# Seven products on six k-tiles instead of four, in a hybrid decoder step on one core

## The chip, the core and the metric

The kernel runs on one core of a Trainium2 chip. What is compared is the device time of one launch in microseconds (us). Of the kernel before there are three timed runs, with a median of 3048.79 us (3048.49 to 3049.93), and one profiled execution of 3050.04 us, whose span from the first to the last instruction is 3048.2 us. Its rows stand below. PE is the matrix engine, PEld its weight loads, DVE the vector engine, ACT the scalar engine, SP the engine that issues the DMAs.

## What is computed

One decoder layer on a prompt of 2048 tokens and on 8 sampled tokens, all in fp32:

```python
xn = rms_norm(x, g_pre)                       # (tokens, 1024)
proj = einsum('bld,de->ble', xn, w_in)        # 1024 -> 11280 columns: the largest product
# columns: q, k, v of 8 delta-rule heads | z_a | a, b | q, k, v of 3 groups x 4 heads | z_b | gates
p_a = gated_delta_rule(silu(conv4(q, k, v)), g, beta) ...  @ w_proj_a
p_b = dilated_window_attention(3 groups)           ...  @ w_proj_b
h   = sigmoid(gate_a) * p_a + sigmoid(gate_b) * p_b
y   = x + rms_norm(h @ w_out, g_post)
```

The outputs are y of both token sets, the final delta-rule states, the last rows before the convolution, and keys and values.

## The kernel before

**Split operands.** Each fp32 operand of a large product is held as two fp32r parts, hi (a cast) and lo (the rest), and a product of a k-tile is three matmuls: hi x hi, hi x lo, lo x hi. In the code this is `three` in `step` (L991).

**The projection.** It is done in two halves of 1024 tokens. The weight columns are cut into 88 tiles of 128, which are worked on in pairs (44 pairs a half; the first pair of half 0 is done plainly in `opening`, with the a/b columns). For a pair the output is a 2 x 2 block: two column tiles by two token groups of 512 (in half 0 each group is done in pieces of 256 and 260 columns, the 4 more being sampled tokens; in half 1 in one piece of 512). The contraction has eight k-tiles of 128. On `KS` = 4 of them the block product is taken with Winograd's seven products of sums instead of eight products, each over `KH = KS // 2` = 2 k-tiles; on the other four (the "rest") it is taken plainly, two column tiles by two token groups. So a pair issues, for each piece, 7 x 2 x 3 = 42 matmuls of the seven products and 4 x 4 x 3 = 48 of the rest. `step` (L983) writes out their order: product 1, the rest that the pair before left over, products 7, 6, 2, rest, 5, 4, rest, 3, rest. In rows `xs1` to `xs7` are the sums of x that the products read, `xp4` to `xp7` the k-tiles of the rest, and `wh`/`wl` the hi and lo parts of the weights.

**What the products need.** On the x side `prep` loads and scales the tokens, `transposed1` and `sums` form the sums of x on DVE, `transpose` turns them on PE, and `xevac` splits them from PSUM (a cast on ACT or DVE, a subtraction on DVE). That is done once a half. On the weight side `wsplit` forms, for each pair, the sums of the weight blocks and splits them (`wput`: a cast on ACT or DVE, a subtraction on DVE) into one of six slots of 512 columns; a slot is freed when its last product is issued (`done` in `step`).

**What sets the order.** The order is settled at build time by a list scheduler (`Scheduler`), which runs generators as tasks with priorities. The projection is the task of lowest priority, and the work on finished tiles (delta rule, attention, gates, sampled tokens) is laid between its matmuls. Tiles are kept in 17 pages of SBUF; claims of pages (`claim`, `admitter`) are granted strictly in the order that the string `ORDER` gives, in which each letter is a delta-rule head, an attention head, a gate tile, and so on. Each engine then executes its own list in that fixed order. After the projection the output products (`final`) run in four token groups.

Of the kernel before, what the change touches and what calls it, by code (L numbers as in the profile page):

```python
# [17 lines left out]
T = 2048  # L18
# [8 lines left out]
KS = 4  # L27
# [426 lines left out]
def build(nc, tc, ctx, I, O):  # L454
# [18 lines left out]
    NPAGE = 17  # L473
# [3 lines left out]
    wslots = Pool([(tl(f"wh{i}", [128, 512], F32R), tl(f"wl{i}", [128, 512], F32R)) for i in range(6)])  # L477
    tbuf = tl("wt", [128, 2 * KH, 128])
# [8 lines left out]
    szg = tl("szg", [128, 12, NB])  # L487
# [79 lines left out]
    def xsamples(pg):  # L567

        page = yield Acquire(pages, 1)
        fxs = page[:, :96].rearrange("p (k t c) -> p k t c", t=2, c=4)  # L570
# [27 lines left out]
    def prep(hf, b, admit):  # L598
# [11 lines left out]
        def scales():  # L610
            st["s2"] = yield Acquire(pages, 1)
            g = I["g_pre"]
            yield K.load(st["s2"][:, :w], bass.AP(tensor=g.tensor, offset=g.offset, ap=[[0, 128], [1, w]]))
# [14 lines left out]
        def scale(i, r):  # L628
            yield K.stt(pg[i][:, :w], pg[i][:, :w], r, st["s2"][:, :w], OP.mult, OP.mult)
            yield K.scaled(pg[i][:, w:D], pg[i][:, w:D], r, ("act",))  # L630
# [57 lines left out]
    def transpose(hf, st, keys, summed=None):  # L688
        pg, m = st["pg"], 128 * KH
        for key in keys:  # L690
            if key[0] in (7, 6, 3):
                yield Wait(summed)
            if hf == 1:
                yield Wait(xfree[key])
            bank = yield Acquire(side, 1)
            if key[0] == "p":
                src = [pg[4 * key[2] + i][:, 128 * key[1]:128 * key[1] + 128] for i in range(4)]
            else:
                n, k = key
                o = 128 * k + m * (n in (2, 3, 4))  # L700
                if n == 6:
                    src = [st["s2"][:, m * i + o:m * i + o + 128] for i in range(4)]
# [30 lines left out]
    def sums(st, ev):  # L733
        m = 128 * KH
        for i in range(4):
            p, q, s2 = st["pg"][i], st["pg"][4 + i], st["s2"][:, m * i:m * i + m]
            a11, a12, s1, a22 = p[:, :m], p[:, m:2 * m], q[:, :m], q[:, m:2 * m]
            yield K.tt(s2, s1, a11, OP.subtract)
            yield K.tt(a11, a22, s2, OP.subtract)
            yield K.tt(a12, a12, s2, OP.subtract)  # L740
        ev.set()

    def transposed1(hf, st, toks):
# [5 lines left out]
        S.spawn(sums(st, ev := Event()), 5, f"sums{hf}")  # L749
# [4 lines left out]
        pages.release(*(pg[i] for i in range(4, 8)), st["s2"])  # L754
        tok.release(*toks, st["toks"][4])
# [3 lines left out]
        if hf == 0:  # L759
            yield Wait(xs_ev[1])  # L760
            pages.release(pg[8])
            tok.release(*st["toks"][5:])
# [25 lines left out]
    def wput(src, ev):  # L788

        hi, lo = slot = yield Acquire(wslots, 1)  # L790
        n = src.shape[1]
        yield K.copy(hi[:, :n], src)
        yield K.tt(lo[:, :n], src, hi[:, :n].bitcast(F32), OP.subtract)
        ev.set(slot)

    def wsplit():
        for at, (kind, us, evs) in enumerate(jobs):
# [4 lines left out]
            if kind == "ab":  # L802
# [3 lines left out]
                slot = yield Acquire(wslots, 1)  # L806
# [5 lines left out]
            elif kind == "plain":  # L812
                m = 128 * KH
                for j in range(2):
                    yield from wput(f[j][:, :2 * m], evs[j])
                    yield from wput(f[j][:, 2 * m:], evs[2 + j])
                T = tbuf.rearrange("p a b -> p (a b)")
                for j in range(2):
                    yield K.tt(T[:, m * j:m * j + m], f[j][:, m:2 * m], f[j][:, :m], OP.subtract)
                yield from wput(T[:, :2 * m], evs[4])  # L820
            elif kind == "pair":
# [3 lines left out]
                T = tbuf.rearrange("p a b -> p (a b)")  # L825
                t1, t2 = (T[:, m * j:m * j + m] for j in range(2))
                yield from wput(f[0][:, :2 * m], evs[0])
                yield K.tt(t1, b12, b11, OP.subtract)
                yield K.tt(b12, b22, b12, OP.subtract)
                yield from wput(f[1][:, :2 * m], evs[1])  # L830
                yield K.tt(t2, b22, t1, OP.subtract)
                yield from wput(T[:, :2 * m], evs[2])
                yield from wput(r1, evs[3])
                yield K.tt(b21, b21, t2, OP.subtract)
                yield from wput(b21, evs[4])
                yield from wput(r2, evs[5])
            else:
                if at < len(jobs) - 2:
                    for j in range(2):
                        yield from wput(f[0][:, 512 * j:512 * j + 512], evs[1 + j])  # L840
# [14 lines left out]
    def sink(t, th, gi, c0, n, bank, pool):  # L855
# [43 lines left out]
        if t.left == 0:  # L899
# [4 lines left out]
            elif k == "z" and t.half == 0:  # L904
                yield K.pcopy(szg[:, t.idx, :], pg[:, HT:HT + NB])
# [21 lines left out]
    def opening(work):  # L927
# [3 lines left out]
        for th in range(2):  # L931
# [36 lines left out]
    def inproj(hf, work):  # L968
# [14 lines left out]
    def step(hf, tiles, evs, slots, gi, c0, w, end, last):  # L983
# [7 lines left out]
        def three(acc, key, hl, off, first, final):  # L991
            hi, lo = (x[:, off:off + 128] for x in hl)
# [5 lines left out]
        def product(acc, n, slot, off, first=False):  # L998
            hl = yield from wk(slot)
            for k in range(KH):  # L1000
                yield from three(acc, (n, k), hl, off + 128 * k, first and k == 0, k == KH - 1)
                if last:
                    if hf == 0:
                        xfree[n, k].set()
                    else:
# [12 lines left out]
        def done(*ns):  # L1018
            if end:
                wslots.release(*(slots[n] for n in ns))  # L1020
# [66 lines left out]
    seb = tl("seb", [128, 2, GH, NB])  # L1087

    def ab_tables(hf, t, work):
# [62 lines left out]
        if hf == 0:  # L1152
# [9 lines left out]
            yield K.copy(seb.rearrange("p a h b -> p (a h b)"), bank[:, :128])  # L1162
            side.release(bank)
        pages.release(ab, pg, tmp, cmat)
# [9 lines left out]
    def conv(t):  # L1174
        pg = yield Wait(t.done)
        cp = yield Acquire(pages, 1)
# [4 lines left out]
        yield K.act(pg[:, :HT], c, AF.Tanh, scale=0.5)  # L1181
        yield K.stt(c, pg[:, :HT], 1.0, c, OP.add, OP.mult)
        pages.release(pg)
        return cp
# [27 lines left out]
    def gdn(hf, h, tk, tq, tv, tz, work, done):  # L1212
# [57 lines left out]
        tok.release(toks.pop())  # L1270
# [3 lines left out]
        tok.release(toks.pop())  # L1274
# [41 lines left out]
    def gdn_q(tq, kT, e, row, sm, tb, h, ev):  # L1316
        qT = yield from conv(tq)
        gp = yield Acquire(pages, 1)
        yield K.load(gp[:, :HT], bass.AP(tensor=row.tensor, offset=row.offset, ap=[[0, 128], [1, HT]]))
# [24 lines left out]
        pages.release(gp)  # L1344
# [385 lines left out]
    def wcols(slot, off, n):  # L1730

        o = off % 512
        return [x[:, o:o + n] for x in slot[off // 512]]
# [182 lines left out]
    def sample_gdn(tiles, abdone):  # L1916
# [25 lines left out]
        pg = yield Acquire(pages, 1)  # L1942
        for i in range(2):
# [42 lines left out]
        for h in range(GH):  # L1986
            S.spawn(sample_head(h, vn, sg_t, pg, kq, qk_b, os_, left, all_done), 15, f"sample{h}")
# [13 lines left out]
        yield K.tt(os_, os_, szg[:, 0:8], OP.mult)  # L2001
# [5 lines left out]
    def sample_head(h, vn, sg_t, pg, kq, qk_b, os_, left, all_done):  # L2007
# [47 lines left out]
    def sample_attn(tiles):  # L2055
# [10 lines left out]
        for h in range(4):  # L2066
            row = brow_d[h, BT:]
            yield K.load(nbs[8 * h:8 * h + 8], bass.AP(
                tensor=row.tensor, offset=row.offset, ap=[[0, NB], [4 * (BT + BS), 3], [1, BS]]))
        slog = pg[:, 908:1004].rearrange("p (g h b) -> p g h b", g=3, h=4)  # L2070
# [79 lines left out]
        yield K.stt(w[0], w[0], 0.5, szg[:, 8:12].rearrange("p h b -> p (h b)"), OP.mult, OP.mult)  # L2150
# [6 lines left out]
    def conv_state():  # L2157
# [13 lines left out]
    ORDER = ("GZaaGaZaGaagZGgaZagGZaagGagagZGagaZGaZagggggggxgyg",  # L2171
             "gGgZggaagGaZSagGaZaGaZgaggGaagTZGaZaCggGaaZgGZaggag")
    for hf in range(2):
# [12 lines left out]
        if hf == 0:  # L2186
            preps = [[claim(7), claim(4)], None]
# [5 lines left out]
        def add_gdn():  # L2193
# [6 lines left out]
            work = claim(4)  # L2200
# [21 lines left out]
        for what in ORDER[hf]:  # L2222
            if what in "GZag":
                {"G": add_gdn, "Z": add_gdn_gate, "a": add_attn, "g": add_gate}[what]()
            elif what == "x":
                preps[1] = [claim(5)]
# [126 lines left out]
```

## Time and profile before

| what | value |
|---|---|
| median of 3 runs | 3048.79 us |
| profiled execution | 3050.04 us |
| its span | 3048.2 us |
| PE busy | 3010.0 us (99%) |
| PEld busy | 2692.0 us (88%) |
| DVE busy | 2199.2 us (72%) |
| ACT busy | 1212.9 us (40%) |

PE is busy nearly all the time in every stage. Busy time of an engine is the union of its instructions' intervals; consecutive matmuls overlap in the records, so the cost of one more matmul is read from the distance of their starts and not from their duration. The projection of half 0 ends at about 1289 us and that of half 1 at about 2560 us; the output products follow.

### The profile page before, as it was taken

Reading aid. Unit: us, or ns where it says so; the run is one execution under the profiler, and the core shown is the slowest. Engines: PE = TensorE matmul, PEld = TensorE weight load, DVE = VectorE, ACT = ScalarE, POOL = GpSimd, SP = SyncE. Lnnn points to the kernel's source line nnn. Section 1 sums busy time; section 2 is a strip of 40 time slices with the busy share of each in tenths; the row PEclk is TensorE's granted clock in tenths of the full one; section 3 lists DMA queues with packets and bytes.
Section 4 is the critical chain, followed back from the end, with each engine's and each line's share of the span. In section 5 each row is a group of like instructions: output and inputs, shape, how many; then the busy total and the mean of one; then the engine's idle time right before and its main releaser. Section 6 shows DMA issues by size and latency. Waiting matters only on the chain.

```text
span 3048.2 us, 55885 instructions
## 1 busy us (share of the span) xinstructions
PE 3010.0 (99%) x20879; PEld 2692.0 (88%) x20879; DVE 2199.2 (72%) x5978; ACT 1212.9 (40%) x3444; POOL 141.1 (5%) x239
## 2 busy tenths in 40 slices
PE   7999999999999999999999999999999999999999
PEld 7999999999999999978887888888888888897887
DVE  6777767786778686767586868597988486666765
ACT  5545444344435443433442534343434343313121
POOL 1000000000000000000000000000000000000000
PEclk9999999999999999999999999999999999999999
DMA  4323242332233325332244332336452236565463
GB/s 125 94 73 89 58 112 71 99 85 83 70 98 89 89 79 147 110 85 81 73 121 124 88 88 80 105 96 186 137 158 86 76 100 180 176 204 197 149 226 117
DMA packets 468760, 343.46 MB, mean 113 GB/s; under 512 B 88745, under 2 KB 411825, under 8 KB 468480
## 3 DMA queue, kind: packets, MB, share of 16 engines
q1 hardware_dynamic: 468488, 339.89, 38.1%
q8 instruction: 164, 2.69, 0.4%
q14 instruction: 108, 0.88, 0.1%
HBM read 261.40 MB, written 80.97 MB: 112 GB/s over the span
## 4 chain that ended last, share of the span: by engine, by line
PE 94%; DVE 3%; DMA 2%; ACT 1%; issue 0%; SPq 0%; POOL 0%; DVEq 0%; POOLq 0%; ACTq 0%
PE bank L251 89%; PE bank L267 5%; DVE pg L311 1%; DMA wr<-in_w_in 0%; DVE wl L316 0%; DVE pg L316 0%; SPq L400 0%; DMA pg<-in_cache_v_w 0%; DMA pg<-in_x_prompt 0%; DMA pg<-in_state_gdn 0%; DMA pg<-gate 0%; ACT L280 0%; DMA ghh<-in_g_head_norm 0%; DVE wh L355 0%; DVE junk L311 0%
## 5 line engine op out<-in xcount | busy, mean ns | idle before, releaser
L280 ACT ACTIVATE pg<-bank 128x256 f32<-128x256 f32 (+7 forms) x741 | 331.8, 460 | 759.4 <-PE bank L251 690.0
L316 DVE TENSOR_TENSOR wl<-wr,wh 128x512 fp32r<-128x512 f32 x595 | 383.5, 647 | 21.3 <-ACT wh L280 3.3
L355 DVE CAST wh<-wr 128x512 fp32r<-128x512 f32 (+1 forms) x384 | 153.0, 399 | 206.9 <-PE bank L251 184.0
L251 PE MATMUL bank<-xp7s,wh 128*128 128x512 f32 (+3 forms) x1196 | 302.1, 328 | 0.0
L251 PE MATMUL bank<-xp6s,wh 128*128 128x512 f32 (+3 forms) x1132 | 290.1, 330 | 0.0
L251 PE MATMUL bank<-xp5s,wh 128*128 128x256 f32 (+3 forms) x1100 | 276.3, 327 | 0.0
L280 ACT ACTIVATE wh<-wr 128x512 fp32r<-128x512 f32 (+1 forms) x213 | 129.8, 611 | 351.9 <-PE bank L251 292.1
L251 PE MATMUL bank<-xp4s,wh 128*128 128x260 f32 (+2 forms) x1068 | 267.5, 326 | 1.6 <-DVE xp4s L311 1.6
L316 DVE TENSOR_TENSOR bank<-bank,etmp 128x256 f32<-128x256 f32 (+2 forms) x260 | 134.9, 519 | 129.4 <-PE bank L251 126.3
L251 PEld LDWEIGHTS bank<-xp7s,wh 128*128 128x128 f32 x1196 | 198.4, 188 | 17.5 <-issue 1.7
L251 PEld LDWEIGHTS bank<-xp6s,wh 128*128 128x128 f32 (+1 forms) x1132 | 189.2, 188 | 17.2 <-issue 0.8
L251 PEld LDWEIGHTS bank<-xp5s,wh 128*128 128x128 f32 (+1 forms) x1100 | 183.0, 188 | 14.7 <-issue 0.2
L251 PE MATMUL bank<-xp7s,wl 128*128 128x512 f32 (+3 forms) x592 | 195.0, 329 | 0.0
L251 PEld LDWEIGHTS bank<-xp4s,wh 128*128 128x128 f32 x1068 | 176.1, 188 | 14.9 <-DVE xp4s L311 1.8
L280 ACT ACTIVATE prob<-bank 128x512 f32<-128x512 f32 (+4 forms) x224 | 105.2, 482 | 208.7 <-PE bank L251 120.8
L311 DVE SCALAR_TENSOR_TENSOR pg<-pg,convw,pg 128x1024 f32<-128x1024 f32 x144 | 183.9, 1277 | 2.8 <-ACT pg L280 1.3
L251 PE MATMUL bank<-xp6s,wl 128*128 128x512 f32 (+2 forms) x560 | 184.9, 330 | 0.0
L251 PE MATMUL bank<-xp5s,wl 128*128 128x512 f32 (+2 forms) x544 | 178.5, 328 | 0.0
L251 PE MATMUL bank<-xs1k,wh 128*128 128x512 f32 (+4 forms) x708 | 177.8, 334 | 0.0
L251 PE MATMUL bank<-xp4s,wl 128*128 128x256 f32 (+2 forms) x528 | 172.5, 327 | 0.0
L251 PE MATMUL bank<-xs6k,wh 128*128 128x512 f32 (+3 forms) x680 | 171.3, 334 | 0.0
L251 PE MATMUL bank<-xs7k,wh 128*128 128x512 f32 (+3 forms) x680 | 169.9, 333 | 0.0
(302 smaller groups left out, 7474.8 us busy)
## 6 DMA issues: line engine op xcount, KB each, us to landing
wr<-in_w_in SPq DMA_DIRECT2D x176, 512.0 KB
pg<-in_x_prompt SPq DMA_DIRECT2D x32, 512.0 KB
pg<-grow SPq DMA_DIRECT2D x32, 512.0 KB
wr<-in_w_proj_a SPq DMA_DIRECT2D x32, 512.0 KB
wr<-in_w_out SPq DMA_DIRECT2D x32, 512.0 KB
pg<-og SPq DMA_DIRECT2D x24, 520.0 KB
pg<-gate SPq DMA_DIRECT2D x24, 512.0 KB
out<-pg SPq DMA_DIRECT2D x20, 512.0 KB
```

The costliest lines, as they stand in the source:

```text
L251: nc.tensor.matmul(out, lhsT, rhs, start=start, stop=stop, skip_group_check=shared)
L267: nc.tensor.transpose(out, in_, ident[:k, :k])
L280: return ("act", c, lambda: nc.scalar.activation(out, in_, func, **kw))
L311: lambda: nc.vector.scalar_tensor_tensor(out, in0, scalar, in1, op0=op0, op1=op1, **kw))],
L316: return ("dve", self._vcost(out, in0, in1), lambda: nc.vector.tensor_tensor(out, in0, in1, op=op))
L355: alts.append(("dve", self._vcost(out, in_, fast=True), lambda: nc.vector.tensor_copy(out, in_)))
```

## The change

`KS` goes from 4 to 6, so each of the seven products runs over three k-tiles and the rest has two. The x sums become 21 rows and the rest 4 (before 14 and 8). The six equal weight slots of 512 columns become three of 768 columns, one of 384 and two of 256, each kind with its own pool, and the scratch `tbuf` is gone: the sums of weights are formed in place in the loaded block. To make room the pages go from 17 to 15, two small tables (`szg`, `seb`) move to DRAM and are loaded where they are used, the convolution works in place over halves of 512 columns with a small buffer instead of a second page, `gdn_q` takes its row from the buffer of the inverse (`lanes`) instead of a page, and a delta-rule head claims 3 pages of work instead of 4, keeping the pages of its q and v. In `sums` the eight subtractions that products 7 and 6 need come first and have an event of their own; the four for product 3 follow. `ORDER` is a new string.

```diff
-KS = 4
+KS = 6
-    NPAGE = 17
+    NPAGE = 15
...
-    wslots = Pool([(tl(f"wh{i}", [128, 512], F32R), tl(f"wl{i}", [128, 512], F32R)) for i in range(6)])
-    tbuf = tl("wt", [128, 2 * KH, 128])
+    wslots, wthird, wrest = Pool([]), Pool([]), Pool([])
+    for i, (pool, w) in enumerate([(wslots, 256 * KH)] * 3 + [(wthird, 128 * KH)] + [(wrest, 128 * (8 - KS))] * 2):
+        pool.free.append((tl(f"wh{i}", [128, w], F32R), tl(f"wl{i}", [128, w], F32R), pool))
...
-    def sums(st, ev):
+    def sums(st, evs):
...
-            yield K.tt(s2, s1, a11, OP.subtract)
-            yield K.tt(a11, a22, s2, OP.subtract)
-            yield K.tt(a12, a12, s2, OP.subtract)
-        ev.set()
+            yield K.tt(s2, q[:, :m], p[:, :m], OP.subtract)
+            yield K.tt(p[:, :m], q[:, m:2 * m], s2, OP.subtract)
+        evs[0].set()
+        for p, q, s2 in tt:
+            yield K.tt(p[:, m:2 * m], p[:, m:2 * m], s2, OP.subtract)
+        evs[1].set()
...
             elif kind == "pair":
...
-                yield K.tt(t1, b12, b11, OP.subtract)
+                yield K.tt(b11, b12, b11, OP.subtract)
                 yield K.tt(b12, b22, b12, OP.subtract)
-                yield from wput(f[1][:, :2 * m], evs[1])
-                yield K.tt(t2, b22, t1, OP.subtract)
-                yield from wput(T[:, :2 * m], evs[2])
-                yield from wput(r1, evs[3])
-                yield K.tt(b21, b21, t2, OP.subtract)
-                yield from wput(b21, evs[4])
-                yield from wput(r2, evs[5])
+                yield from wput([f[1][:, :2 * m]], evs[1])
+                yield K.tt(b22, b22, b11, OP.subtract)
+                yield from wput([b11, b22], evs[2])
+                yield from wput([r1], evs[3], wrest)
+                yield K.tt(b21, b21, b22, OP.subtract)
+                yield from wput([b21], evs[4], wthird)
+                yield from wput([r2], evs[5], wrest)
...
     def conv(t):
...
-        c, w = cp[:, :HT], convw[:, t.idx]
-        yield K.scaled(c, pg[:, 3:3 + HT], w[:, 3:4])
-        for i in (2, 1, 0):
-            yield K.stt(c, pg[:, i:i + HT], w[:, i:i + 1], c, OP.mult, OP.add)
+        for o in (0, HT // 2):
+            c = yield Acquire(prob_t, 1)
+            yield K.scaled(c, pg[:, o + 3:o + 3 + HT // 2], w[:, 3:4])
+            for i in (2, 1, 0):
+                yield K.stt(c, pg[:, o + i:o + i + HT // 2], w[:, i:i + 1], c, OP.mult, OP.add)
...
-        gp = yield Acquire(pages, 1)
+        ln = yield Acquire(lanes, 1)
+        gp = ln[0]
...
-            work = claim(4)
+            work = claim(3)
...
-    ORDER = ("GZaaGaZaGaagZGgaZagGZaagGagagZGagaZGaZagggggggxgyg",
+    ORDER = ("GaaGZgaaZGaaGZGZagagGZaagGaaZggGaagZGgagZagggggxgyg",
```

On PE, in a pair of half 0, product 4 and the rest that follows it on the same bank. Before:

```order
L251 MATMUL bank_67<-xs4k_79,wh_118 128x256 x2
L251 MATMUL bank_67<-xs4k_79,wl_119 128x256
L251 MATMUL bank_67<-xs4k_80,wh_118 128x256 x2
L251 MATMUL bank_67<-xs4k_80,wl_119 128x256
L251 MATMUL bank_67<-xp4s_87,wh_120 128x256
L251 MATMUL bank_67<-xp4s_88,wh_120 128x256
L251 MATMUL bank_67<-xp4s_87,wl_121 128x256
L251 MATMUL bank_67<-xp5s_89,wh_120 128x256
L251 MATMUL bank_67<-xp5s_90,wh_120 128x256
L251 MATMUL bank_67<-xp5s_89,wl_121 128x256
```

And of the change, the same product and its rest:

```order
L251 MATMUL bank_67<-xs4k_82,wh_121 128x256 x2
L251 MATMUL bank_67<-xs4k_82,wl_122 128x256
L251 MATMUL bank_67<-xs4k_83,wh_121 128x256 x2
L251 MATMUL bank_67<-xs4k_83,wl_122 128x256
L251 MATMUL bank_67<-xs4k_84,wh_121 128x256 x2
L251 MATMUL bank_67<-xs4k_84,wl_122 128x256
L251 MATMUL bank_67<-xp6s_94,wh_123 128x256
L251 MATMUL bank_67<-xp6s_95,wh_123 128x256
L251 MATMUL bank_67<-xp6s_94,wl_124 128x256
L251 MATMUL bank_67<-xp7s_96,wh_123 128x256
L251 MATMUL bank_67<-xp7s_97,wh_123 128x256
L251 MATMUL bank_67<-xp7s_96,wl_124 128x256
```

Before, two k-tiles of product 4 and four of the rest stand here (xp6 and xp7 follow in the same way); of the change, three and two.

On DVE, in an early pair of half 0, the slot that products 6 and 5 read; `wt` and `wr` hold sums of weights, `lane` and `sm` belong to other work. Before it is one cast and one subtraction of 512 columns:

```order
L316 TENSOR_TENSOR wl_117<-wr_112,wh_116 128x512
L316 TENSOR_TENSOR wt<-wr_112,wt 128x256
L316 TENSOR_TENSOR lane_t<-lane_t,lane_x 128x8x9
L355 CAST wh_122<-wt 128x512
L316 TENSOR_TENSOR lane_x<-lane_w,lane_t 128x64
L316 TENSOR_TENSOR wl_123<-wt,wh_122 128x512
```

Of the change it is two of each, of 384 columns, behind the reciprocal and scalings of another head:

```order
L316 TENSOR_TENSOR sm_142<-sm_142,tkdg 128x4
L299 TENSOR_SCALAR pg_98<-bank_69,sm_142 128x128 x2
L355 CAST wh_117<-wr_114 128x384
L311 SCALAR_TENSOR_TENSOR pg_103<-bank_70,sm_141,pg_103 128x128
L316 TENSOR_TENSOR wl_118<-wr_114,wh_117 128x384
L355 CAST wh_117<-wr_113 128x384
L299 TENSOR_SCALAR sm_142<-sm_142 128x8
L311 SCALAR_TENSOR_TENSOR pg_103<-bank_70,sm_141,pg_103 128x128
L316 TENSOR_TENSOR wl_118<-wr_113,wh_117 128x384
L316 TENSOR_TENSOR wl_124<-wr_114,wh_123 128x256
```

The cast of a slot stands in DVE's list where PE frees the slot, so it waits there for PE, with the rows behind it.

## Rows read from the trace of the kernel before

**Rows 1.** Page, part 1: busy us (share of the span) xinstructions

```profile
PE 3010.0 (99%) x20879; PEld 2692.0 (88%) x20879; DVE 2199.2 (72%) x5978; ACT 1212.9 (40%) x3444; POOL 141.1 (5%) x239
```

**Rows 2.** Waits of PE: us in total, times, longest us

```profile
PE bank L267 <- DVE ssx L301: 8.5, 1, 8.5
PE bank L267 <- DVE xs1k L316: 5.2, 2, 2.8
PE bank L267 <- DVE pg L316: 3.1, 2, 1.7
PE bank L251 <- DVE st L311: 2.7, 6, 1.1
```

**Rows 3.** Chain of waits, two unbroken pieces of half 0: start us, us, what

```profile
869.47 45.09 PE bank L251 x379
...
1154.65 47.50 PE bank L251 x399
```

**Rows 4.** Timeline of PE in half 1: start us, us, instructions xcount

```profile
1999.65 0.62 PE L251 MATMUL bank<-xp6s,wh 128*128 128x512 f32 x2
2000.11 0.40 PE L251 MATMUL bank<-xp6s,wl 128*128 128x512 f32 x1
...
2009.38 0.62 PE L251 MATMUL bank<-xp6s,wh 128*128 128x512 f32 x2
```

**Rows 5.** Timeline of PE where other work is laid between

```profile
2010.07 0.40 PE L251 MATMUL bank<-xp7s,wh 128*128 128x512 f32 x1
2010.31 0.60 PE L267 MATMUL bank<-cst,pg 128*128 128x128 f32 x4
2010.67 0.48 PE L251 MATMUL bank<-xp7s,wh 128*128 128x512 f32 x1
2010.98 0.40 PE L251 MATMUL bank<-xp7s,wl 128*128 128x512 f32 x1
```

**Rows 6.** DVE groups by form: xcount | busy us, mean ns | idle before, releasers

```profile
L316 DVE TENSOR_TENSOR wl<-wr,wh 128x512 fp32r<-128x512 f32 x508 | 347.0, 686 | 20.2 <-ACT wh L280 3.3 <-PE bank L251 2.3
L311 DVE SCALAR_TENSOR_TENSOR pg<-pg,convw,pg 128x1024 f32<-128x1024 f32 x144 | 183.9, 1277 | 2.8 <-ACT pg L280 1.3
L355 DVE CAST wh<-wr 128x512 fp32r<-128x512 f32 x314 | 133.0, 423 | 197.2 <-PE bank L251 175.2 <-DMA wr<-in_w_out 11.0 <-DMA wr<-in_w_in 3.8
L316 DVE TENSOR_TENSOR wl<-wr,wh 128x256 fp32r<-128x256 f32 x87 | 36.5, 420 | 1.0
L355 DVE CAST wh<-wr 128x256 fp32r<-128x256 f32 x69 | 19.8, 287 | 9.7 <-PE bank L251 8.8
```

**Rows 7.** Stretches of 50 us: length, busy of PE, PEld, DVE, ACT, POOL, PEclk, DMA

```profile
1250.00:1300.00 50.00, 46.92 (x331) 43.65 (x330) 41.85 (x86) 24.14 (x48) 2.15 (x3) 0.97 0.38 124
2000.00:2050.00 50.00, 50.00 (x281) 42.61 (x280) 48.74 (x131) 24.03 (x66) 0.60 (x1) 1.00 0.37 105
2300.00:2350.00 50.00, 46.63 (x241) 38.93 (x241) 42.47 (x115) 24.16 (x73) 2.01 (x2) 0.90 0.38 109
```

**Rows 8.** Stretches of 10 us between the halves, and half 1 nearly whole

```profile
1270.00:1280.00 10.00, 7.42 (x56) 6.61 (x54) 9.61 (x22) 5.13 (x11) 0.00 (x0) 1.00 0.32 110
1280.00:1290.00 10.00, 9.49 (x63) 8.90 (x64) 8.82 (x16) 7.96 (x14) 0.00 (x0) 0.83 0.25 62
...
1290.00:2550.00 1260.00, 1254.20 (x7206) 1038.22 (x7205) 938.74 (x2718) 494.63 (x1327) 55.10 (x82) 0.99 0.38 105
```

**Rows 9.** Timeline of DVE while the sums of half 0 are made

```profile
43.79 2.34 DVE L316 TENSOR_TENSOR pg<-pg,pg 128x256 f32<-128x256 f32 x6
47.05 1.29 DVE L316 TENSOR_TENSOR xs7k<-bank,xs7k 128x512 fp32r<-128x512 f32 x2 [0.92 <-ACT xs7k L280]
48.26 1.28 DVE L316 TENSOR_TENSOR xs6k<-bank,xs6k 128x512 fp32r<-128x512 f32 x2
```

More of the change, by code (lines that the diff above doesn't have):

```diff
@@ L486, in build @@
     snew_d = dr.tile([128, 24, NB], F32, name="snew_d")
[L487 removed]
+    szg_d = dr.tile([128, 12, NB], F32, name="szg_d")
+    seb_d = dr.tile([128, 2 * GH * NB], F32, name="seb_d")
+    seb_ev = Event()
     ssm = tl("ssm", [128, 3, 12, NB])
@@ L610, in scales @@
         def scales():
-            st["s2"] = yield Acquire(pages, 1)
+            st["s2"] = yield Acquire(pages, 2)
             g = I["g_pre"]
-            yield K.load(st["s2"][:, :w], bass.AP(tensor=g.tensor, offset=g.offset, ap=[[0, 128], [1, w]]))
+            yield K.load(st["s2"][0][:, :w], bass.AP(tensor=g.tensor, offset=g.offset, ap=[[0, 128], [1, w]]))
         def squares(i, r, acc):
@@ L701, in transpose @@
                 if n == 6:
-                    src = [st["s2"][:, m * i + o:m * i + o + 128] for i in range(4)]
+                    src = [st["s2"][i // 2][:, m * (i % 2) + o:m * (i % 2) + o + 128] for i in range(4)]
                 else:
@@ L753, in transposed1 @@
         yield from transpose(hf, st, keys, ev)
-        pages.release(*(pg[i] for i in range(4, 8)), st["s2"])
-        tok.release(*toks, st["toks"][4])
+        pages.release(*(pg[i] for i in range(4, 8)), *st["s2"])
+        tok.release(*toks, *st["toks"][4:6])
         yield Wait(st["done0"])
@@ L786, in wload, with wput @@
             raw_ev.set(raw)
[L788 to L793, printed above, removed]
+    def wput(parts, ev, pool=wslots):
+        hi, lo, _ = slot = yield Acquire(pool, 1)
+        c = 0
+        for src in parts:
+            v = slice(c, c := c + src.shape[1])
+            yield K.copy(hi[:, v], src)
+            yield K.tt(lo[:, v], src, hi[:, v].bitcast(F32), OP.subtract)
         ev.set(slot)
@@ L1004, in product @@
                         xfree[n, k].set()
+                    elif k == 2 and n < 4:
+                        x = XS[n][k]
+                        wslots.release((x[:, 0:512], x[:, 512:1024], wslots))
                     else:
@@ L1019, in done @@
             if end:
-                wslots.release(*(slots[n] for n in ns))
+                wfree(*(slots[n] for n in ns))
         t1, t2 = tiles
@@ L1317, in gdn_q @@
         qT = yield from conv(tq)
-        gp = yield Acquire(pages, 1)
-        yield K.load(gp[:, :HT], bass.AP(tensor=row.tensor, offset=row.offset, ap=[[0, 128], [1, HT]]))
+        ln = yield Acquire(lanes, 1)
+        gp = ln[0]
+        yield K.load(gp, bass.AP(tensor=row.tensor, offset=row.offset, ap=[[0, 128], [1, HT]]))
         qk = e
@@ L1343, in gdn_q @@
         yield K.tt(qT[:, :HT], qT[:, :HT], gp[:, :HT], OP.mult)
-        pages.release(gp)
+        lanes.release(ln)
         ev.set((qT, qk))
@@ L1732, in wcols @@
         o = off % 512
-        return [x[:, o:o + n] for x in slot[off // 512]]
+        return [x[:, o:o + n] for x in slot[off // 512][:2]]
     def three(w, x, n, s0, sn):
@@ L1942, in sample_gdn @@
         pg = yield Acquire(pages, 1)
+        seb = pg[:, 256:384].rearrange("p (a h b) -> p a h b", a=2, h=GH)
+        szg = pg[:, 384:448].rearrange("p (h b) -> p h b", h=GH)
+        yield Wait(seb_ev)
+        yield K.load(pg[:, 256:384], seb_d)
+        yield K.load(szg, szg_d[:, 0:8])
         for i in range(2):
```

81 lines of the change are left out of this document (41 added, 40 removed).

## The prediction

> **What bounds the kernel now.** I read the page's busy times first: PE 3010.0 us of a span of 3048.2, DVE 72%, ACT 40% [rows 1]. Then the waits of PE: they are few, the largest at the start (8.5 us for the first scaled tile, 5.2 us for the first split of x), and the recurrence of the delta rule takes the rest in pieces of about 1 us [rows 2]. What PE doesn't spend busy is 3048.2 - 3010.0 = 38.2 us, and no other engine is near its limit over the whole. So PE bounds the kernel, and the number of matmuls times their distance is its time. The distance is read from the timeline, since records overlap: in half 0 two unbroken pieces of the chain have 379 matmuls in 45.09 us and 399 in 47.50 us, 119 ns each (moving widths of 256 and 260) [rows 3]. In half 1, from 1999.65 to 2009.38 us there are 42 matmuls of 512 columns, nothing between them: 9.73 / 42 = 231.7 ns [rows 4]. In both, the distance goes with the width of the moving operand and not with waits, so a matmul less is that much less, if PE stays fed.
>
> [...]
>
> **The change part by part.** *Matmuls removed.* A pair has 42 + 48 = 90 matmuls a piece before, and 7 x 3 x 3 + 4 x 2 x 3 = 63 + 24 = 87 after. Half 0 has 43 such pairs in two pieces: 258 fewer, x 119 ns = 30.7 us. Half 1 has 44 pairs in one piece: 132 fewer, x 231.7 ns = 30.6 us. Together 61.3 us. The opening, the a/b columns, the output products and all the work between keep their matmuls.
>
> *Matmuls added.* Three more rows of x a half are turned on PE, four transposes each: 24. Four stand from 2010.31 to 2010.67, 90 ns each [rows 5], so 2.2 us.
>
> *Places where PE turns from projection to other work.* In that place the matmul after the transposes is followed after 0.31 us instead of 0.23, so a return costs about 0.08 us [rows 5]. The order of the change has 1089 such blocks of other work, that of before 1039: 50 x 0.08 = 4.0 us more.
>
> So PE alone: -30.7 - 30.6 + 2.2 + 4.0 = -55.1 us. All of it is on the path, since PE is.
>
> *DVE.* By its rows a subtraction takes 686 ns at 512 columns and 420 at 256, 1.04 ns a column, and a cast 423 and 287, 0.53 ns a column [rows 6]. Per pair the sums of weights grow by 4 x 128 columns and the splits by 3200 - 2816 = 384 columns: (512 + 384) x 1.04 = 0.93 us, and the casts, of which DVE has about two thirds, 0.13 us; together about 1.1 us on 87 pairs, 96 us. The convolution makes eight calls of 512 columns where it had four of 1024 (48 of them): 2 x 686 - 1277 = 95 ns a time [rows 6], four times, 18 us, and its scalings some 5 us. DVE goes from 2199 to about 2320 us of some 3000, 77%. This lies beside PE as long as nothing in it is late. In half 1 it has 938.7 us of 1260 now [rows 8], 74%; with 44 x 1.1 + 12 = 60 us more in some 1230 it is 81%. That 81% as such needn't cost PE: from 2000 to 2050 us DVE is busy 48.74 us and PE all 50.00 [rows 7]. I take nothing for the mean load, with 25 us as the upper end (the second rival).
>
> *The start.* Scaling a tile is 768 columns wide instead of 512 (0.27 us more, four tiles before the second part of the opening), the first slots are 768 wide (0.27 + 0.13 us more before the first matmul). PE waits for DVE there already [rows 2], so I take 2 us, between 0 and 8.
>
> *Between the halves.* From 1270 to 1290 us PE loses 3.1 us, DVE is 92% busy and the granted clock is 0.83 in the second 10 us [rows 8], so this stretch hangs on DVE. More there: 16 sums of 384 instead of 256 columns (16 x 0.13 = 2.1 us), eight wider scalings (2.1 us) and three more splits of x (3 x 0.69 = 2.1 us). Of these 6.3 us a part goes beside the transposes. Against it stands the new order of the sums: in half 0 DVE waited 0.92 us for the first row of product 7 right behind the last sum [rows 9], and now the four sums for product 3 stand in DVE's list between, so PE turns product 7's rows meanwhile. I take 4 us, between -3 (the present loss gone) and 10.
>
> *Weight slots.* The slot of products 6 and 5 was the one that product 4 of the pair before freed; now it is one of three wide ones, freed by product 3. In between PE had 12 + 6 + 12 + 6 + 12 + 6 = 54 projection matmuls, 6.4 us in half 0; now it has the rest (6), product 1 (9), the left-over rest (6) and product 7 (9), that is 30, 3.57 us, plus what is laid between. In that time DVE must make two casts and two subtractions of 384 columns, 2 x 0.36 + 2 x 0.55 = 1.8 us, and with two other calls of about 0.34 between them 2.5 us. It fits with 1 us to spare in half 0 and 4.6 us in half 1, where the same 30 matmuls take 6.95 us. I take 3 us for the pairs where it doesn't, between 0 and 60 (the third rival).
>
> *Pages, DMA.* Two pages fewer against smaller claims. In the order of the change fewer than 60 other matmuls stand in a row without a projection matmul until the projection ends, so nowhere does the projection wait long for a page; nothing taken, 10 us as the upper end. Some 16 small DMAs go to SP's queue; what stands behind them there are loads of work that has slack. At the end 313 of the other matmuls are left when the projection ends, against 112; among them is a piece of some 2.5 steps of the recurrence with no output product between, and such a step's waits are now up to 1.1 us each [rows 2]: 1.5 us, between 0 and 5.
>
> **The sum.** 3050.04 (profiled) - 55.1 + 2 + 4 + 3 + 1.5 = 3005.4. The median of the runs shown is 1.25 us under the profiled one, so 3004 us.
>
> **The rivals.** *Cleaner than I think (0.10).* The added DVE work lies in gaps and the present stalls go down with the new order: 3048.8 - 55.1 = 2994 us, or a few less. For it speaks that PE had hardly a wait in 50-us stretches where DVE is full; against it the stretch between the halves.
>
> *DVE binds in places of half 1 (0.14).* Where DVE is full already, 48.74 of 50 us [rows 7], 5% more work makes it late, sinks empty the banks late and PE waits. Five stretches of half 1 that lose 5 us each give 25 us: about 3029 us. Against it: the scheduler lays other work where a matmul isn't ready, and the work is spread anew.
>
> *Slower: the wide slot is late in every pair of half 0 (0.08).* DVE executes its list in order, and the cast of a slot stands there waiting for PE: 175.2 of the 197.2 us of idle time before these casts are waits for PE [rows 6]. If two long calls (768-column subtractions, about 0.95 us by the slope) come between, the chain is 2.5 + 1.9 + 0.3 = 4.7 us against 3.57, and each of 43 pairs loses 1.1 us, 47 us. PE then idles in every pair, and the clock goes with it, as it did from 2300 to 2350 us (0.90 after 3.4 us of idle [rows 7]), some 15 us more: 3004 + 62 = 3066 us. It decides from 3.57 us of that chain upwards. Against it: the 768-column split of the slot for product 7 has its slot 15 k-tiles earlier and should be done by then.
>
> [...]
>
> **How the numbers follow.** Forecast, 2998 to 3014 us, 0.66; the cleaner case 0.10; DVE in half 1 0.14; the slower case 0.08; 0.02 for more than one of these together. The range that should hold the time 8 times in 10 takes in the clean case's and most of the DVE case's: 2989 to 3034 us. What a measurement here can tell from no change is 0.2%, 6 us: faster means under 3042.7, slower over 3054.9. The forecast, the clean case and most of the DVE case are faster (0.88), the DVE case's upper end is the same (0.04), the rest slower (0.08).
>
> **What would show it.** PE's busy time at 2955 us or so, with 20513 or so instructions (366 fewer matmuls); the unbroken distances again at 119 and 232 ns; PE's idle time between 38 and 55 us, the growth at the start and between the halves; DVE at about 2320 us. Waits of PE's L251 on `wl` of DVE L316, of which there are none among the first rows now, would show the late slot. The forecast is wrong if PE's idle time grows by more than 25 us, or if the distance of the matmuls changes.

## The result and the profile after

The changed kernel takes 2996.03 us (median of 4 runs, 2993.75 to 2997.31) against 3049.11 us (4 runs, 3048.49 to 3049.93): a ratio of 0.9825 [0.9808, 0.9842], 53 us less. The forecast was 3004 us, 8 us too high. The time lies inside the range, but 2 us below the forecast's own 2998 to 3014 us: the clean rival's 2994 us is nearer.

The profiled execution takes 2993.75 us, its span 2992.0 us, 56.2 us less than before. Busy time of the engines, the line that answers to [rows 1]:

```profile
PE 2952.5 (99%) x20513; PEld 2636.8 (88%) x20513; DVE 2352.0 (79%) x6283; ACT 1238.0 (41%) x3620; POOL 125.9 (4%) x228
```

PE has 57.5 us and 366 instructions less, and its idle time goes from 38.2 to 39.5 us: the gain is PE work that is no longer there, and nothing came in its place. DVE has 153 us more and the span doesn't show it. The waits of PE of the changed kernel (us in total, times, longest us) are those of [rows 2] again; the late weight slot, `wl` for L251, is far down with 0.5 us:

```profile
PE bank L267 <- DVE ssx L301: 9.1, 1, 9.1
PE bank L267 <- DVE pg L316: 6.0, 4, 3.2
PE bank L267 <- DVE xs1k L316: 4.3, 2, 3.2
PE bank L251 <- DVE st L311: 1.6, 4, 0.7
...
PE bank L251 <- DVE wl L316: 0.5, 2, 0.3
```

Unbroken pieces of the chain after (start us, us, what), against [rows 3, 4]: 25.14 / 212 = 118.6 ns and 31.22 / 263 = 118.7 ns in half 0, 23.85 / 103 = 231.6 ns in half 1. The distances of the matmuls are those of before.

```profile
508.25 25.14 PE bank L251 x212
1072.12 31.22 PE bank L251 x263
1258.06 23.85 PE bank L251 x103
```

Idle time by stage is read from long windows (length, then busy us of PE, PEld, DVE, ACT, POOL, then granted clock and DMA). Before, the start, half 0 and the end, for the rest see [rows 8]:

```profile
0.00:50.00 50.00, 33.66 (x252) 30.88 (x252) 39.09 (x107) 30.21 (x73) 11.55 (x30) 1.00 0.48 141
50.00:1270.00 1220.00, 1214.14 (x10781) 1200.91 (x10779) 881.37 (x2507) 555.73 (x1766) 60.28 (x108) 1.00 0.32 91
...
2550.00:3048.00 498.00, 491.08 (x2532) 406.44 (x2530) 321.59 (x612) 119.19 (x254) 14.14 (x19) 1.00 0.55 184
```

And after:

```profile
0.00:50.00 50.00, 35.35 (x244) 33.48 (x245) 39.33 (x99) 27.21 (x77) 11.34 (x31) 0.93 0.50 143
50.00:1230.00 1180.00, 1177.91 (x10522) 1164.37 (x10521) 957.03 (x2651) 564.56 (x1855) 55.39 (x96) 1.00 0.34 94
1230.00:1250.00 20.00, 14.00 (x92) 12.64 (x92) 19.79 (x40) 7.53 (x17) 0.00 (x0) 0.84 0.28 86
1250.00:2500.00 1250.00, 1241.00 (x7146) 1025.25 (x7145) 1010.15 (x2874) 517.55 (x1411) 46.57 (x82) 0.99 0.38 107
2500.00:2992.00 492.00, 484.24 (x2517) 401.07 (x2515) 325.71 (x623) 121.11 (x261) 12.65 (x19) 1.00 0.55 184
```

PE's idle time (length less busy) changes by -1.7 us at the start, -3.8 in half 0, +2.9 between the halves, +3.2 in half 1 and +0.8 at the end. At the start less idle time isn't less time, since the granted clock there is 0.93 against 1.00: after the same 208 instructions of PE, product 5 of the first pair (`xs5k`) starts at 45.77 us where it started at 44.60. Between the halves, from the last matmul of half 0 to product 7 of half 1, PE has the same 20 transposes, and 10.7 us pass instead of 7.1 (start us, us, instruction; before, then after):

```profile
44.60 0.40 PE L251 MATMUL bank<-xs5k,wh 128*128 128x256 f32 x2
...
1276.49 0.29 PE L251 MATMUL bank<-xp7s,wl 128*128 128x260 f32 x1
...
1283.85 0.48 PE L251 MATMUL bank<-xs7k,wh 128*128 128x512 f32 x1
```

```profile
45.77 0.40 PE L251 MATMUL bank<-xs5k,wh 128*128 128x256 f32 x2
...
1239.52 0.28 PE L251 MATMUL bank<-xp7s,wl 128*128 128x260 f32 x1
...
1250.47 0.48 PE L251 MATMUL bank<-xs7k,wh 128*128 128x512 f32 x1
```

Between the halves DVE is busy 19.79 of 20 us: that stretch hangs on DVE more than before. In half 1 DVE is busy 81% of the time, and PE idles 9.0 us there.

### The profile page after: what moved, and what is told of

It is laid out like the page before. It is cut to its first block, busy times and chain, and to the rows that moved or that the text cites. A ratio compares the mean times of both kernels' runs of the same rounds, so it can differ in the third digit from the quotient of the medians.

```text
span 2992.0 us, 55631 instructions
## 1 busy us (share of the span) xinstructions
PE 2952.5 (99%) x20513; PEld 2636.8 (88%) x20513; DVE 2352.0 (79%) x6283; ACT 1238.0 (41%) x3620; POOL 125.9 (4%) x228
## 4 chain that ended last, share of the span: by engine, by line
PE 93%; DVE 3%; issue 2%; DMA 1%; ACT 0%; SPq 0%; POOL 0%; DVEq 0%; POOLq 0%; ACTq 0%
PE bank L251 88%; PE bank L267 5%; DVE wl L316 1%; DVE pg L311 0%; DVE wr L316 0%; DVE junk L311 0%; DMA wr<-in_w_in 0%; DVE wh L355 0%; DMA pg<-in_state_gdn 0%; SPq L400 0%; DVE pg L316 0%; DVE prob L311 0%; DMA lane_t<-in_c_consts 0%; DMA pg<-ya_d 0%; DVE lane_x L316 0%
## 5 line engine op out<-in xcount | busy, mean ns | idle before, releaser
L280 ACT ACTIVATE pg<-bank 128x256 f32<-128x256 f32 (+9 forms) x735 | 332.2, 465 | 634.0 <-PE bank L251 575.6
L316 DVE TENSOR_TENSOR wl<-wr,wh 128x384 fp32r<-128x384 f32 (+3 forms) x693 | 433.5, 635 | 16.1 <-ACT wh L280 4.9
L251 PE MATMUL bank<-xp7s,wh 128*128 128x256 f32 (+4 forms) x1116 | 282.6, 327 | 0.0
L251 PE MATMUL bank<-xp6s,wh 128*128 128x256 f32 (+3 forms) x1092 | 276.7, 328 | 0.0
L251 PE MATMUL bank<-xs7k,wh 128*128 128x512 f32 (+3 forms) x910 | 226.5, 332 | 0.0
L251 PE MATMUL bank<-xs6k,wh 128*128 128x512 f32 (+3 forms) x894 | 223.2, 331 | 0.5 <-ACT bank L280 0.5
L251 PE MATMUL bank<-xs1k,wh 128*128 128x512 f32 (+5 forms) x894 | 221.3, 333 | 0.0
L311 DVE SCALAR_TENSOR_TENSOR prob<-pg,convw,prob 128x512 f32<-128x512 f32 x288 | 214.3, 746 | 3.8
L251 PE MATMUL bank<-xs2k,wh 128*128 128x256 f32 (+5 forms) x878 | 215.2, 327 | 0.0
L251 PE MATMUL bank<-xs5k,wh 128*128 128x260 f32 (+4 forms) x846 | 203.0, 326 | 0.0
L251 PEld LDWEIGHTS bank<-xp7s,wh 128*128 128x128 f32 (+1 forms) x1116 | 185.8, 188 | 15.8 <-issue 0.8
L251 PE MATMUL bank<-xs4k,wh 128*128 128x256 f32 (+4 forms) x822 | 195.7, 325 | 0.0
L251 PEld LDWEIGHTS bank<-xp6s,wh 128*128 128x128 f32 (+1 forms) x1092 | 181.2, 188 | 15.6 <-issue 1.7
L251 PE MATMUL bank<-xs3k,wh 128*128 128x256 f32 (+2 forms) x792 | 193.2, 328 | 0.0
L251 PE MATMUL bank<-xp7s,wl 128*128 128x512 f32 (+3 forms) x552 | 181.6, 329 | 0.0
L251 PE MATMUL bank<-xp6s,wl 128*128 128x256 f32 (+2 forms) x540 | 176.9, 328 | 0.0
L251 PEld LDWEIGHTS bank<-xs7k,wh 128*128 128x128 f32 x910 | 152.6, 190 | 12.5 <-issue 0.8
```

The costliest lines, as they stand in the source:

```text
L251: nc.tensor.matmul(out, lhsT, rhs, start=start, stop=stop, skip_group_check=shared)
L280: return ("act", c, lambda: nc.scalar.activation(out, in_, func, **kw))
L311: lambda: nc.vector.scalar_tensor_tensor(out, in0, scalar, in1, op0=op0, op1=op1, **kw))],
L316: return ("dve", self._vcost(out, in0, in1), lambda: nc.vector.tensor_tensor(out, in0, in1, op=op))
```

## The experiments

The first theory was the prediction's: PE bounds, a matmul saved is its distance saved, and everything else in the change nets nearly zero. The rivals: the order and pages gave part of the gain, or DVE holds part of it back. Each experiment is the changed kernel with one edit, in some with another ORDER or number of pages besides; ratios are to the kernel before, run beside it.

**Four k-tiles again, with all the rest of the change** (e1_ks4: new pages, claims, order of the sums, convolution).

```diff
-KS = 6
+KS = 4
...
-    for i, (pool, w) in enumerate([(wslots, 256 * KH)] * 3 + [(wthird, 128 * KH)] + [(wrest, 128 * (8 - KS))] * 2):
+    for i, (pool, w) in enumerate([(wslots, 256 * KH)] * 3 + [(wthird, 384)] + [(wrest, 128 * (8 - KS))] * 2):
...
-                    elif k == 2 and n < 4:
+                    elif k == KH - 1 and n < 4:
```

> The changed code with KS = 4: seven products on four k-tiles as before, with all the rest of the change (15 pages, smaller claims, convolution in place, new ORDER, sums in the new order; the three rows that become weight slots at the end are those of the second k-tile). Theory (PE is bound by its matmuls, one to one): 390 matmuls come back (258 x 119 ns + 132 x 231.7 ns = 61.3 us), 24 transposes go (2.2 us): 2996 + 59 = 3055 us, and against the kernel before within 6 us. Rival (the new pages, claims and ORDER carry part of the gain): clearly under the kernel before, for instance 3030 us. Other rival (they cost something that the seven products pay for): 3065 us or more.

3050.86 us, ratio 1.000 [0.9992, 1.0009]. All the other edits together are worth nothing here, and the whole gain appears with the six k-tiles: 0.0175 of 3050 us, 53 us, where the terms of the matmuls gave 61.3 - 2.2 = 59 us. One reserve: e1 keeps the string of the changed kernel, so four k-tiles with a string of their own could be faster than 3050.86 us. That the gain is matmuls rests as much on PE's busy time, 57.5 us less at unchanged distances and idle time.

**The sums in their old order** (e2_oldsums).

```diff
-        evs[0].set()
-        for p, q, s2 in tt:
             yield K.tt(p[:, m:2 * m], p[:, m:2 * m], s2, OP.subtract)
+        evs[0].set()
         evs[1].set()
```

> The changed kernel with the sums of x in the order of before (tile by tile, one event behind all twelve subtractions). Theory (the order of the sums fills DVE's wait for the first row of product 7 once a half, about 0.9 us in half 0): 2997 to 2998 us. Rival (it is what keeps the stretch between the halves short): 3000 to 3005 us.

2997.14 us, ratio 0.9824 [0.9810, 0.9837]: no difference that can be told. Its row between the halves has 1.3 us less of PE than the changed kernel's, with a lower clock (0.74 against 0.84), so the new order helps there, if at all, by 1 to 2 us (in the traces 10.7 us pass from half 0's last matmul to product 7, here 12.2):

```profile
1230.00:1250.00 20.00, 12.73 (x75) 11.07 (x74) 18.42 (x38) 7.15 (x16) 0.00 (x0) 0.74 0.28 86
```

**The ORDER of the kernel before** (e3_oldorder).

```diff
-    ORDER = ("GaaGZgaaZGaaZGZagagGZaagGaaZggGaagZGgagZagggggxgyg",
-             "GZgaaggGagSagZgGaaZGaggZaGagagTgZGggaZagGaaGZaZggaC")
+    ORDER = ("GZaaGaZaGaagZGgaZagGZaagGagagZGagaZGaZagggggggxgyg",
+             "gGgZggaagGaZSagGaZaGaZgaggGaagTZGaZaCggGaaZgGZaggag")
```

> The changed kernel with the ORDER string of before, so the same work with other claims of pages in turn. Theory (PE-bound with slack in the pages): PE busy 2952 us within 5, time 2996 to 3010 us. Rival (15 pages bind unless the order is fitted to them): PE idle grows by more than 25 us, 3020 us or more.

3134.89 us, ratio 1.0277 [1.0261, 1.0293]: 139 us slower than the changed kernel with the same 20513 PE instructions. The theory of this run fell. Its page line:

```profile
PE 3032.2 (97%) x20513; PEld 2681.9 (86%) x20513; DVE 2341.4 (75%) x6244; ACT 1255.1 (40%) x3659; POOL 133.8 (4%) x228
```

Of the 136 us between the spans (3127.7 against 2992.0) only 56 are idle time of PE; 80 us lie in its busy time. The windows show how. From 1682 us on PE has the recurrence of the delta rule and little else; the clock is granted at 0.50, PE counts as busy 90 to 99%, and DVE is idle for most of it:

```profile
1680.00:1690.00 10.00, 9.04 (x41) 7.13 (x40) 1.40 (x4) 1.14 (x3) 0.00 (x0) 0.50 0.20 55
1690.00:1700.00 10.00, 9.95 (x41) 8.32 (x39) 3.54 (x13) 1.94 (x9) 0.00 (x0) 0.50 0.00 1
1700.00:1710.00 10.00, 9.62 (x25) 5.56 (x24) 4.62 (x16) 1.02 (x6) 1.20 (x2) 0.50 0.00 0
```

The timeline of PE there (start us, us, instructions, idle before and releaser) has steps of the recurrence and no product of the projection, until product 1 starts at 1717.16 us, 36.7 us after the last one. It isn't the only such stretch: from 50 to 2500 us nine of over 10 us lie between two projection matmuls, 164 us together, where the changed kernel has one, of 10.7 us (between the halves).

```profile
1711.37 0.80 PE L251 MATMUL bank<-rr,pg 128*128 128x128 f32 x2
1712.59 1.22 PE L251 MATMUL bank<-ww,pg 128*128 128x128 f32 x4 [0.43 <-ACT ww L280]
1713.83 1.22 PE L251 MATMUL bank<-st,pg 128*128 128x128 f32 x4
1715.07 0.80 PE L251 MATMUL bank<-rr,pg 128*128 128x128 f32 x2
1716.29 1.22 PE L251 MATMUL bank<-ww,pg 128*128 128x128 f32 x4 [0.43 <-ACT ww L280]
1717.16 1.20 PE L251 MATMUL bank<-xs1k,wh 128*128 128x512 f32 x2
```

PE's busy time alone doesn't tell this stretch from full work: from 1690 to 1700 us 9.95 us of 10 are counted as busy, at a granted clock of 0.50. The new theory: a finished tile needs a page, pages are granted strictly in the order of the string, and where the string doesn't fit the times at which heads give pages back, the projection stands still behind a claim until a recurrence has run out. Pages, not only PE, bound the kernel then.

**82 us of matmuls less, ORDER kept** (e4_droplo: of the last k-tile of the rest the third matmul, lo x hi, is left out, 520 matmuls, 81.7 us by the distances).

```diff
-            for j, (a, x) in enumerate(((hi, xh), (hi, xl), (lo, xh))):
+            n3 = 2 if key[0] == "p" and key[1] == 7 else 3
+            for j, (a, x) in enumerate(((hi, xh), (hi, xl), (lo, xh))[:n3]):
...
```

> The changed kernel without the lo x hi matmul of the last k-tile of the rest (that small part of the projection is left out), DVE's work unchanged: 43 x 2 x 4 = 344 matmuls of half 0 and 44 x 4 = 176 of half 1 go. Theory (still one to one): 344 x 119 ns + 176 x 231.7 ns = 81.7 us, 2996 - 82 = 2914 us. Rival (DVE at 79% is the next bound): half of that or less, 2950 us or more, with PE idle up by 30 us or more.

3028.19 us, ratio 0.9926 [0.9913, 0.9938]: less work, and 32 us slower than the changed kernel. The clock is 0.974, and PE's waits for `ww` (total, times, longest) rise from 1.3 us to 15.4, as in e3 (14.0):

```profile
PE bank L251 <- ACT ww L280: 15.4, 37, 0.8
```

So the theory fell, and by this run alone its rival, DVE, could stand. The reading to test: a faster projection moves the times at which tiles come, and the string no longer fits.

**The same with an ORDER fitted to it** (e7_droplo_refit: e4 with a string chosen anew at build time for this kernel).

> The kernel of the run that left out the lo x hi matmul of the last k-tile of the rest (81.7 us of matmuls, slower by 32 us than the changed kernel), with an ORDER fitted to it. Theory A (pages and the turn of claims took the gain): 2915 to 2945 us, PE's waits for ww, rr and st back under 10 us together. Theory B (DVE or the recurrence binds beyond this point whatever the order): 2980 us or more.

2933.99 us, ratio 0.9609 [0.9593, 0.9625]: 62 us under the changed kernel of the 82 (66 by the two ratios to the kernel before). PE's waits for `ww`, `rr` and `st` are 5.3 us together: theory A held. Page lines of e4 and of e7:

```profile
PE 2947.5 (97%) x19993; PEld 2613.7 (86%) x19993; DVE 2340.4 (77%) x6236; ACT 1252.3 (41%) x3667; POOL 124.6 (4%) x228
```

```profile
PE 2886.5 (98%) x19993; PEld 2572.4 (88%) x19993; DVE 2323.8 (79%) x6226; ACT 1254.8 (43%) x3677; POOL 129.6 (4%) x228
```

The same matmuls cost 61 us less of busy time. So a matmul saved is worth its distance, mostly, but only with a string that fits.

**Pages by themselves** (e5_ks4_old15 and e6_ks4_old18: e1 with the ORDER of before, with 15 and with 18 pages).

```diff
-    NPAGE = 15
+    NPAGE = 18
```

> The changed code with KS = 4 and the ORDER of before, 15 pages. Theory A (the pages are a second bound beside PE: claims are granted in ORDER's turn, a projection tile that has no page holds its bank, and PE is left with the recurrence alone): even without the seven products on six k-tiles the old ORDER is slow on 15 pages, 3085 us or more, against 3051 with the new ORDER. Theory B (what made the old ORDER slow was only its fit to the six k-tiles): 3050 to 3060 us.

> The same (KS = 4, ORDER of before) with 18 pages, for which there is room at KS = 4. Theory A (pages): most of the loss comes back, 3050 to 3065 us. Theory B (not the pages): the same time as with 15.

3120.94 us, ratio 1.0220 [1.0206, 1.0235], and 3067.64 us, ratio 1.0046 [1.0030, 1.0063]: with the same instructions three pages more give back 53 us of the 67 by which e5 is slower than the kernel before. Theory A held for e5; e6 is 2.6 us above its range. In the windows of half 1 of e5 and of e6, PE issues 182 matmuls more in the same 1300 us with the pages:

```profile
1250.00:2550.00 1300.00, 1274.74 (x7177) 1051.86 (x7176) 953.81 (x2800) 517.19 (x1388) 47.43 (x84) 0.96 0.36 99
```

```profile
1250.00:2550.00 1300.00, 1289.65 (x7359) 1066.36 (x7360) 972.90 (x2901) 533.65 (x1432) 51.01 (x85) 0.98 0.37 102
```

Stretches of over 10 us without a projection matmul, five in e5 with 100 us, are two in e6 with 39 us. So too few pages for the string make e3's kind of loss; with pages enough the string matters less. That a page claim is what the projection stands behind is no row of a trace (it is settled when the kernel is built); it is inferred from e5 and e6. More pages with six k-tiles were not tried.

**DVE loaded with 74 us of calls more** (e8_dvemore: the last subtraction of each pair is done twice again, with the same values).

```diff
                 yield from wput([r2], evs[5], wrest)
+                for _ in range(2):
+                    hi, lo, _s = evs[5].val
+                    yield K.tt(lo[:, :256], r2, hi[:, :256].bitcast(F32), OP.subtract)
```

> The changed kernel with the last weight subtraction of each pair (256 columns) done two times more: 174 calls of 0.42 us, some 60 us of DVE's time in the weight task. Theory A (DVE at 79% isn't the bound; its load lies beside PE): 2996 to 3010 us. Theory C (DVE's load, or its part in the weight task, is close to binding, or shifts the turn of pages): 3030 us or more.

3058.14 us, ratio 1.0013 [1.0003, 1.0024]: the whole gain is gone. The 174 calls take 73.9 us (the 60 us expected were 174 x 0.42 us, wrongly multiplied), and DVE's busy time grows by 64 us, as some other work leaves it. Taken alone that reads as a DVE bound. But its windows show the stretch of e3 again, 36 us without a projection matmul up to 951.63 us, and in these 20 us of it DVE is idle for most of the time:

```profile
920.00:930.00 10.00, 8.00 (x36) 6.44 (x36) 4.95 (x10) 2.70 (x6) 0.00 (x0) 0.52 0.34 87
930.00:940.00 10.00, 8.85 (x28) 6.20 (x27) 2.22 (x7) 2.19 (x11) 0.38 (x1) 0.50 0.00 0
```

**The same load with an ORDER fitted to it** (e9_dvemore_refit).

> The two repeated subtractions a pair of e8 (some 60 us of DVE more, same matmuls), with an ORDER fitted to this kernel; the outputs' values don't change. Theory: DVE's load as such doesn't bind; e8 lost 62 us because the turn in which pages are granted no longer fitted the times at which the work came. With a fitted ORDER the time is within 15 us of the changed kernel, 2990 to 3012 us, with PE's waits for ww back below 2 us and the granted clock back at 0.99. Rival: DVE at 79% and more binds in places, whatever the order: 3035 us or more.

2995.13 us, ratio 0.9818 [0.9804, 0.9833]: that of the changed kernel, with the same calls still there (DVE's busy time 51 us above the changed kernel's). Half 1 of e8 and of e9:

```profile
1250.00:2500.00 1250.00, 1222.11 (x7049) 1008.51 (x7047) 1038.51 (x2913) 516.44 (x1401) 47.26 (x83) 0.98 0.37 104
```

```profile
1250.00:2500.00 1250.00, 1241.27 (x7184) 1028.44 (x7185) 1043.28 (x2947) 532.46 (x1451) 46.78 (x83) 0.99 0.39 107
```

DVE is as busy in both (83%), PE has 135 matmuls more in e9. The waits for `ww` fall from 4.9 to 0.9 us and the clock is 0.994 again. The stretches of over 10 us are three with 68 us in e8, one with 14 us in e9. DVE doesn't bind, not even nearly 3 points above its load in the changed kernel's half 1; e8's loss was the string's.

**Less load on DVE** (e10_poolrest_refit: the subtraction of the 256-column slots on POOL, with an ORDER fitted to it; e11_poolrest: with the ORDER of the changed kernel).

```diff
-            yield K.tt(lo[:, v], src, hi[:, v].bitcast(F32), OP.subtract)
+            tt = K.ptt if pool is wrest else K.tt
+            yield tt(lo[:, v], src, hi[:, v].bitcast(F32), OP.subtract)
```

> The subtraction of the slots of the rest (256 columns, two a pair) on POOL instead of DVE, with an ORDER fitted to it. Theory: PE bounds the changed kernel, so some 75 us less of DVE's work gives back only what PE idles for it, 0 to 8 us: 2986 to 2998 us. Rival 1: DVE binds in places of half 1: 2975 us or less. Rival 2: POOL is slower at this and makes the slots late, or disturbs DVE: 3005 us or more, with waits of PE's L251 for wl of POOL.

> As e10, with the ORDER of the changed kernel left as it is. Theory: less load on DVE, but a turn of pages that no longer fits: slower than e10 by 10 us or more, 3000 to 3040 us. Rival: the ORDER fits a smaller load as well as it does the larger: within 5 us of e10.

3000.81 us, ratio 0.9830 [0.9814, 0.9846], not to be told from the changed kernel, and 3018.79 us, ratio 0.9890 [0.9877, 0.9904], some 20 us slower. So relieving DVE gives nothing, and even a lighter load with the string unchanged costs. The theory of e11 held; e10 is 3 us above what its theory gave and 4 us under what its second rival did; in its trace product 5 of the first pair starts at 48.23 us, 2.5 us later than in the changed kernel's. No version here that computes everything is shown to beat the changed kernel. POOL's form (xcount, busy us, mean ns, idle before), and one on DVE of the changed kernel and of e10:

```profile
L367 POOL TENSOR_TENSOR wl<-wr,wh 128x256 fp32r<-128x256 f32 x176 | 156.5, 889 | 1396.7 <-ACT wh L280 881.6 <-PE bank L251 228.4 <-DVE wh L355 65.1
```

```profile
L316 DVE TENSOR_TENSOR wl<-wr,wh 128x384 fp32r<-128x384 f32 x263 | 145.1, 552 | 4.3 <-ACT wh L280 0.9
```

```profile
L316 DVE TENSOR_TENSOR wl<-wr,wh 128x384 fp32r<-128x384 f32 x263 | 151.9, 577 | 3.2
```

POOL takes 889 ns where DVE took 418, and DVE's busy time fell by 16 us only, though 73.6 us of calls left it: other work came to it, and some of its calls on SBUF became longer (these from 552 to 577 ns, those of 768 columns from 951 to 958 only), while a call of 512 columns that works in PSUM stayed at 693 ns. The last section shows which ones.

## Why the prediction was right, and where it was not

*PE bounds, and the matmuls are the gain.* Right. PE's busy time fell by 57.5 us (55.1 forecast), instructions and distances are those forecast, and in e1 the whole gain goes with the six k-tiles (with the reserve made there). Weight loads are busy 88% of the time after as before. With the order fitted, 82 us of matmuls less were worth 62 us (e7): not quite one for one, and the clock there is 0.990 against 0.994.

*The stalls.* Here most of the forecast's excess lies. Between the profiled executions it is 11.7 us (3005.4 against 2993.75): 2.4 us in PE's busy time and 9.2 in its idle time, which was to grow by 2 + 4 + 3 + 1.5 = 10.5 us and grew by 1.3. (The median lies 2.3 us above the profiled execution, not 1.25 us under it, so 8 us are left there.) Two of the terms were well sized all the same: the start is 1.2 us longer in this trace (2 forecast; in e3, e8 and e9, with the same 208 instructions, 0 to 0.4 us), and the stretch between the halves 3.6 us (4 forecast). The slots were not: PE waits 0.5 us for them, not 3, and idles 2.1 us in all of half 0, where the slower rival (each pair late) had 47 us. The end idles 0.8 us more (1.5 forecast). And half 0 has 3.8 us less idle time than before, which no term had, half 1 3.2 us more. That these come out near nothing together is partly luck.

*DVE.* Its growth was mis-sized, 153 us against some 120, and most of the difference lies in the convolution. Its calls in the small buffer take 746 ns, where 686, the subtraction's, was assumed: 288 of them take 214.3 us, 30.4 more than the 144 before, where 18 were forecast. And its scalings on DVE went from 7.5 to 26.1 us, as DVE now has 54 of them instead of 10, where some 5 us were taken. The step that this costs PE nothing held: e9 has still more of it and the same time. The rival that DVE binds in half 1 is refuted by e8 and e9 together; e8 alone would have confirmed it.

*Pages: nothing taken, 10 us as the upper end.* The value was right for this kernel and the bound was not one: with the string of before the same code on the same 15 pages takes 139 us more (e3), and e5 and e6 show the same kind of loss without the six k-tiles. The change escapes that because its string fits its pages and durations. The step's reason, fewer than 60 other matmuls in a row, is a weak measure: in the trace of the changed kernel 68 stand in a row from 1521 us on and take 7.0 us, while 20, between the halves, come with 10.7 us, and 122 in e3 with 36.7, at half the clock and each step waiting for the one before. What tells the runs apart are the stretches of over 10 us between two projection matmuls, read from the timelines from 50 to 2500 us (in e7 to the projection's end at 2437 us). They hold other work, so not all of their time is lost.

| run | median us | stretches | together us |
|---|---|---|---|
| before | 3049.11 | 1 | 20 |
| changed | 2996.03 | 1 | 11 |
| e1 | 3050.86 | 1 | 10 |
| e3, string of before | 3134.89 | 9 | 164 |
| e4, string kept | 3028.19 | 9 | 211 |
| e7, e4 with its string | 2933.99 | 1 | 23 |
| e5, 15 pages | 3120.94 | 5 | 100 |
| e6, 18 pages | 3067.64 | 2 | 39 |
| e8, string kept | 3058.14 | 3 | 68 |
| e9, e8 with its string | 2995.13 | 1 | 14 |

The kernel before has one too, from 2302.9 us on, with 82 matmuls. It lies in the stretch of clock 0.90 in [rows 7], which the prediction read as 3.4 us of idle time alone: the sign that a string can leave PE with the recurrence was there to see.

Open: which of its letters make a string fit, and how much of the 16 to 20 us that e7 doesn't give back is string and how much PE's other waits.

## What to carry to other kernels

Where a build-time order and a strict turn of buffers are fitted to a kernel, any edit that changes durations, even one that removes work, can cost more than it saves until they are fitted again (e4, e8, e11); an experiment that keeps the old order measures the misfit together with the edit. Fit the order for every variant before a bound is named. Read the granted clock beside busy time: the stretches of e3 and e8 with PE 80 to 99% busy at about 0.50 and DVE mostly idle were chains of dependent small matmuls, not work at the limit.

## What the hardware showed unexpectedly

PE's busy time for one and the same number of matmuls was 2952.5 us in the changed kernel and 3032.2 us in e3: at a granted clock of 0.50 the intervals are longer (a group of four `ww` matmuls 1.22 us in e3, 0.71 in the kernel before at 2303.10 us, where the granted clock was 1.00) and fill the waits of the recurrence (9.95 us of 10 are busy from 1690 to 1700 us of e3).

And in e10 DVE's calls on SBUF took longer where an instruction of POOL overlapped them. Casts of 384 columns went from 353 to 386 ns on the mean, but 162 of them, which no instruction of POOL overlaps, still take 353 ns; the other 41 take 515 ns, up to 907. Subtractions of 384 columns take 552 ns alone (170) and 625 beside POOL (93), the convolution's calls 747 (247) and 880 (41). Calls of 256 columns that read and write PSUM take 427 ns alone and 426 beside POOL (18). One such pair on DVE, and POOL's instructions at that time (start us, us, instruction):

```profile
335.18 0.75 DVE L311 SCALAR_TENSOR_TENSOR prob<-pg,convw,prob 128x512 f32<-128x512 f32 x1
336.31 1.22 DVE L311 SCALAR_TENSOR_TENSOR prob<-pg,convw,prob 128x512 f32<-128x512 f32 x1
```

```profile
336.20 0.78 POOL L367 TENSOR_TENSOR wl<-wr,wh 128x256 fp32r<-128x256 f32 x1 [2.57 <-ACT wh L280]
336.93 0.65 POOL L382 COPY halo<-pg 128x3 f32<-128x3 f32 x1
```

The call that POOL's two instructions overlap takes 1.22 us, the one of the same form before it 0.75. Why the calls on SBUF became longer beside POOL, and those of 256 columns that read and write PSUM did not (426 ns against 427), no run here shows.
